# Queueing the sums of activated chunks behind the splits of the next three weight pieces

## The chip, the core and the metric

The kernel runs on one core of a Trainium2 chip. The metric is the device time of one execution in microseconds (us). Engine names are those of the profile: PE is TensorE (matmuls), PEld its weight loads, DVE is VectorE, ACT is ScalarE, POOL is GpSimd, and SP is SyncE, whose queue issues nearly all DMAs.

## What is computed

The reference is a trunk of two layers over 256 tokens of width 1024, in float32. Each layer has a token mixer (pooling, dilated attention, gates) and an MLP with a width-3 convolution over the tokens on the activated branch. The change touches the MLP alone:

```python
def _conv_ffn(xn, w_up, conv_w, conv_b, w_down):
    a, gval = jnp.split(xn @ w_up, 2, axis=-1)
    a = lax.conv_general_dilated(a, conv_w[:, None, :], ...) + conv_b
    return (jax.nn.gelu(a) * gval) @ w_down

def reference(x, ...):
    h = x
    for layer in range(DEPTH):
        h = h + _token_mixer(_rmsnorm(h, norm1[layer]), ...)
        h = h + _conv_ffn(_rmsnorm(h, norm2[layer]), w_up[layer], ...)
    return _rmsnorm(h, norm_f)
```

The inner width of the MLP is 2816, or 22 chunks of 128 columns.

## The kernel before

**Split weights.** Every weight is loaded in float32 and split on the chip into a high part `wh` (a rounding copy on ScalarE, L201) and a low part `wl` (the difference, on VectorE, L199). A matrix product is then three products: high by high, low by high and high by low. The class `Weights` does this for a fixed list of *pieces*, each 128 partitions by 1024 elements. A load brings two pieces (1024 KB). Three buffers hold raw loads and five hold split pieces (`RAW, BUFS, LOOK = 3, 5, 3`, L104). `W.get` (L218) hands out the next piece and, before that, has the pieces up to three further on split (`_split`, L158, and `open_next`, L178); `W.free` gives a piece back. A load is issued on SP as soon as a raw buffer is free, unless it is held behind another DMA (`loads_behind`, L134).

**The order.** The program is written as one stream. The compiler's scheduler places each instruction in the in-order queue of its engine, and where the stream leaves it free it may place an instruction ahead of an earlier one. `tc.issue_after(inst)` binds this: what is written inside the block and runs on the engine of `inst` is queued behind `inst`, with no wait of its own.

**The MLP's steps.** The activated branch of chunks 0 to 3 is made by rows of tokens and turned round through memory (a "crossing"); from chunk 4 on, `up` (L1249) projects each chunk by itself. The value branch is made in groups of four chunks by `by_halves` (L1233) and crosses too; the last two chunks have theirs projected (L1269). From chunk 4 on the main loop (L1316) goes by pairs of chunks, nine pairs per layer:

- at chunks 4, 8, 12 and 14, half a value group: two pieces (`HALF_GROUPS`, L42), 24 matmuls at L654;
- `up(f)` and `up(f + 1)`: two pieces, 32 matmuls at L530, drawn together by `proj(x2, 2)` (L538); then the activation of each;
- from chunk 6 on, two steps of the down projection (`residual_mm`, L576), for chunks f - 6 and f - 5 (`LAG = 6`): two pieces, 24 matmuls at L572 to L574.

So the pieces run: values, 4, 5, 6, 7, down, down, values, values, 8, 9, down, down, 10, 11, and so on.

**A chunk's sum.** A projection writes one PSUM bank: the wide matmuls (`wh`, 512 columns) fill both halves and the narrow ones (`wl`, 256 columns) add to the second. `two_sums` (L517) runs the wide ones first in one pair and the narrow ones first in the next. `add_up` (L564) fetches the second half with a copy on ScalarE (L566), then adds the first half to it on VectorE (L567). Behind that come the convolution and the gelu, three more operations on ScalarE (L1259, L1273, L1277) and five on VectorE (L1260, L1263, L1274, L1278, L1282), and the split of the result (L1293, L1294). The banks come from a pool of four (`mmp`, L237), which the value products share; a half-finished value group keeps two.

When `up(4)` has drawn pieces 4 and 5, the splits of 6, 7 and the first down piece stand ahead of `add_up` in the stream. In the queues they need not.

Of the kernel before, what the change touches and what calls it, by code (L numbers as in the profile page):

```python
# [10 lines left out]
F32 = mybir.dt.float32  # L11
# [85 lines left out]
class Weights:  # L97
# [8 lines left out]
    def __init__(self, tc, pool, idle):  # L106
        self.tc, self.nc, self.pool, self.idle = tc, tc.nc, pool, idle
        self.loads, self.pieces = [], []
        self.n_loaded, self.n_split, self.n_got = 0, 0, 0
        self.raw, self.split = {}, {}  # L110
        self.live = set()
        self.behind, self.later = (), []
        self.loads_behind = {}
        self.n_scaled, self.gains = 0, None

# [10 lines left out]
    def load(self, upto):  # L126
        while self.n_loaded < min(upto, len(self.loads)):
            src, shape, tag = self.loads[self.n_loaded]
            name = f"raw{self.n_loaded}"
            if tag is None:  # L130
                t = self.pool.tile([P, *shape], F32, tag="raw", bufs=self.RAW, name=name)
            else:
                t = self.idle.tile([P, *shape], F32, tag=tag, name=name)
            held = self.loads_behind.get(self.n_loaded)  # L134
            with self.tc.issue_after(held.ins) if held else ExitStack():
                self.last = self.nc.sync.dma_start(out=t, in_=src)
            self.raw[self.n_loaded] = t
            self.n_loaded += 1

# [38 lines left out]
    def open_next(self):  # L178


        nc, i = self.nc, self.n_split
        n, cut, shape, slot = self.pieces[i]
        if slot is None:
            self.live.add(i)
            h, l = (
                self.pool.tile([P, *shape], F32R, tag=tag, bufs=self.BUFS, name=f"{tag}{i}")
                for tag in ("wh", "wl")
            )
        else:
            tag, part, of = (*slot, 0, 1)[:3]  # L190
            if part == 0:
                self.shared = self.idle.tile([P, of, 2, *shape], F32R, tag=tag, name=f"{tag}{i}")
            h, l = self.shared[:, part, 0], self.shared[:, part, 1]
        src = cut(self.raw[n])
        self.split[i] = (h, l)
        self.n_split += 1
        if i >= self.n_scaled:
            def rest():
                self.last_rest = nc.vector.tensor_sub(out=l, in0=src, in1=h.bitcast(F32))  # L199

            return [(lambda: nc.scalar.copy(out=h, in_=src), rest)]  # L201

        def scaled(j):
            k = (i * shape[0] + j) % KD
            g = self.gains[:, k : k + 1]
            return (
                lambda: nc.scalar.activation(h[:, j], src[:, j], AF.Copy, scale=g),
                lambda: nc.vector.scalar_tensor_tensor(
                    out=l[:, j], in0=src[:, j], scalar=g, in1=h[:, j].bitcast(F32),
                    op0=ALU.mult, op1=ALU.subtract,  # L210
                ),

                lambda: nc.vector.tensor_scalar_mul(h[:, j], src[:, j], g),
            )

        return [scaled(j) for j in range(shape[0])]

    def get(self, look=LOOK):  # L218
        i = self.n_got
        self.n_got += 1  # L220
        self._split(i + 1 + look)
        return i, self.split[i]

    def free(self, i):
        self.live.discard(i)
# [3 lines left out]
def encoder(ctx, tc, x, w_in, w_pool, pool_scale, w_a, w_b, w_o, norm1, norm2, w_up, conv_w,  # L229
            conv_b, w_down, rel_bias, norm_f, onehot, edges, out):  # L230
    nc = tc.nc
# [9 lines left out]
    W = Weights(tc, wpool, big)  # L241
# [18 lines left out]
    for l in range(DEPTH):  # L260
# [36 lines left out]
        for f in range(4, NF, 2):  # L297
            if f in HALF_GROUPS:
                n, j = HALF_GROUPS[f]
                W.use(rows(w_up[l], j * 512, 4, DFF + n * 512, 512))  # L300
            a = cols(w_up[l], f * P)
            if f >= 4 * NQ:
                g = cols(w_up[l], DFF + f * P)
                a = [a[0], g[0], a[1], g[1]]
# [7 lines left out]
    h = const.tile([P, 2, D], F32, name="h")  # L312
# [225 lines left out]
    def proj(x2, n=1):  # L538


        if not ready:
            pieces = [W.get() for _ in range(n)]
            ps = [mmp.tile([P, 2, S], F32, tag="mm", name="proj_ps") for _ in range(n)]
            two_sums(
                x2, KD,
                *(
                    (b, lambda k, wh=wh: wh[:, k, :], lambda k, wl=wl: wl[:, k, :])
                    for b, (_, (wh, wl)) in zip(ps, pieces)
                ),
            )  # L550
            for i, _ in pieces:
                W.free(i)
            ready.extend((b[:, 0], b[:, 1]) for b in ps)
        return ready.pop(0)

    def halves(a):

        return a.rearrange("p (t m) -> p t m", t=2)

    def in_order(a):  # L560

        return a.rearrange("p (m t) -> p t m", t=2)

    def add_up(out, sums):  # L564

        nc.scalar.copy(out=out, in_=sums[1])  # L566
        nc.vector.tensor_add(out=out, in0=sums[0], in1=out)  # L567
# [322 lines left out]
    for l in range(DEPTH):  # L890
# [21 lines left out]
        if l == 0:  # L912
            with tc.manual_schedule():
                begun = begin_values_of_x()
            x2 = first_values(*begun, keep_values)
        else:
            for g in range(NG):
                held = begun[0] if g == 0 else [W.get() for _ in range(4)]
                for t in range(2):
                    if g + t == 0:  # L920
                        ps = begun[1]
                    else:
                        ps = v_tile()
# [16 lines left out]
        for gi in range(3, -1, -1):  # L940
            w = WINDOWS[gi]
            u = sm.tile([P, 2, S + 2 * PAD], F32, tag="u", name="u")
            nc.vector.memset(u[:, :, 0:PAD], 0.0)
            nc.vector.memset(u[:, :, PAD + S :], 0.0)
            for j in range(2):
                if l == 0 and (gi, j) == (1, 0):

                    with tc.issue_after(W.last.ins):
                        next(bias)
                add_up(in_order(u[:, j, PAD : PAD + S]), [halves(a) for a in proj(x2, 1 + (l > 0))])  # L950
            cur, n = u, S + 2 * PAD
            sh = 1
            while sh < w:
                nxt = sm.tile([P, 2, S + 2 * PAD], F32, tag="us", name="us")
                n -= sh
                nc.vector.tensor_add(
                    out=nxt[:, :, 0:n], in0=cur[:, :, 0:n], in1=cur[:, :, sh : sh + n]
                )
                cur = nxt
                sh *= 2  # L960
            hw = w // 2
            o = PAD - hw
            e = edge[:, gi, 0:hw].unsqueeze(1).to_broadcast([P, 2, hw])
            nc.vector.tensor_mul(out=cur[:, :, o : o + hw], in0=cur[:, :, o : o + hw], in1=e)
            if hw > 1:
                e = edge[:, gi, hw : w - 1].unsqueeze(1).to_broadcast([P, 2, hw - 1])
                r = slice(o + S - hw + 1, o + S)
                nc.vector.tensor_mul(out=cur[:, :, r], in0=cur[:, :, r], in1=e)
            pd = sm.tile([P, 2, S], F32, tag="us", name="pd")
            nc.vector.scalar_tensor_tensor(  # L970
                out=pd, in0=cur[:, :, o : o + S], scalar=1.0 / w, in1=u[:, :, PAD : PAD + S],
                op0=ALU.mult, op1=ALU.subtract,
            )
            both = pl2[gi // 2][:, gi % 2 * 2 : gi % 2 * 2 + 2]
            ph, pl = both[:, :, 0], both[:, :, 1]
            pd = pd.rearrange("p k (m t) -> p k t m", t=2)
            nc.scalar.copy(out=ph, in_=pd)
            nc.vector.tensor_sub(out=pl, in0=pd, in1=ph.bitcast(F32))
            pooled[gi] = both
# [122 lines left out]
        for m, c in enumerate(PAIRS):  # L1102
# [7 lines left out]
            for n in range(4):  # L1110
                if m == 1:
                    next(pool_parts)
                src, rest = (halves(a) for a in proj(x2, 1 + (m != 1)))
                hd = 2 * c + n % 2
                scale = HD**-0.5 if n < 2 else 1.0
                if hd < HPG:
# [3 lines left out]
                        out=lo[:, hd], in0=src, scalar=scale, in1=hi[:, hd].bitcast(F32),  # L1120
# [3 lines left out]
                        out=lo[:, hd], in0=rest, scalar=scale, in1=lo[:, hd].bitcast(F32),  # L1124
                        op0=ALU.mult, op1=ALU.add,
                    )
                else:
# [3 lines left out]
                        out=o, in0=src, scalar=scale, in1=o, op0=ALU.mult, op1=ALU.add  # L1131
# [6 lines left out]
        for cc in HALVES:  # L1138
            ps = by_tokens(po2, 4, then=step)
# [10 lines left out]
        for cc in HALVES:  # L1150
# [4 lines left out]
            for t in range(2):  # L1155
                nc.vector.scalar_tensor_tensor(
                    out=pa[:, t, cc], in0=th[:, t], scalar=1.0, in1=pa[:, t, cc],
# [6 lines left out]
        for n, cc in enumerate(HALVES):  # L1164
            th = gate()
            ps = by_tokens(at2, 2, 2)
# [25 lines left out]
        x2 = two_parts("x", "x2")  # L1192
# [33 lines left out]
        def to_z(ps, z, but, after):  # L1226
            y = big.tile([P, 2, 4, 4, 32], F32, tag="v0", name="crossing")
            cross(ps, y, z, "crossing", but, after)
# [4 lines left out]
        def by_halves(n):  # L1233
            ps = by_tokens(x2, 4, end=2)
            yield
            by_tokens(x2, 4, ps=ps, begin=2)
            to_z(ps, z_of[n % 3], 0, W.last_rest)
            yield

        held, ps0 = entry  # L1240
# [8 lines left out]
        def up(f):  # L1249
            w0, w1, w2, b = (prm[:, l, j * NF + f : j * NF + f + 1] for j in range(4))  # L1250
            a = sm.tile([P, S], F32, tag="u", name="a")
            if f < 4:
                nc.scalar.copy(
                    out=a.rearrange("p (a j t) -> p t a j", t=2, j=32), in_=of_chunk(za, f)
                )
            else:
                add_up(in_order(a), [halves(b) for b in proj(x2, 2)])
            y = sm.tile([P, S], F32, tag="s", name="y")
            nc.scalar.activation(y, a, AF.Identity, bias=b, scale=w1)  # L1259
            nc.vector.scalar_tensor_tensor(  # L1260
# [99 lines left out]
```

## Time and profile before

| | us |
|---|---|
| runs shown, median of 3 (lowest to highest) | 879.88 (879.86 to 880.11) |
| profiled execution, its own time | 881.7 |
| its span, first to last instruction | 879.9 |
| PE busy | 857.7 (97%) |
| PEld busy | 731.4 (83%) |
| DVE busy | 663.8 (75%) |
| ACT busy | 495.7 (56%) |

The mean granted TensorE clock is 0.991 of full speed. Times in the timeline count from the span's start. A timeline row gives the start, how long the merged instructions took, the engine, the line, the operation with output and input, the count, and in brackets the idle time before it with what ended it. The MLP of layer 0 runs from about 250 to 440 us, that of layer 1 from about 684 us to the end.

### The profile page before, as it was taken

How to read it: one execution, taken by the hardware profiler on the slowest of the kernel's cores; microseconds unless marked ns; L12 is line 12 of the kernel's file. 1: busy time of each engine (PE TensorE's matmuls, PEld its weight loads, DVE VectorE, ACT ScalarE, POOL GpSimd, SP SyncE). 2: the span in 40 equal slices, each digit the busy share in tenths (PEclk: the TensorE clock that was granted, in tenths of full speed). 3: DMA queues.
4: the chain of work that ended last, by engine and by line, in shares of the span. 5: the costliest groups of instructions: out<-in, count | busy, mean ns of one | idle time of the engine just before them, and what ended most of it. 6: DMA issues, size and time to landing. Idle time of an engine off the chain costs nothing.

```text
span 879.9 us, 11813 instructions
## 1 busy us (share of the span) xinstructions
PE 857.7 (97%) x4343; PEld 731.4 (83%) x4343; DVE 663.8 (75%) x1050; ACT 495.7 (56%) x795; POOL 31.7 (4%) x98
## 2 busy tenths in 40 slices
PE   9999999999999789999999999999999997999997
PEld 7888888888888678888888888988888886788886
DVE  7998797567677587879856987783687685787894
ACT  7756554455455466667645675453554563565673
POOL 1800000000000000000000000000000000000000
PEclk9999999999999989999999999999999998999999
DMA  9676555766848637657726564747865686466741
GB/s 333 208 244 209 182 191 199 256 233 227 297 145 283 220 131 252 239 192 239 239 96 217 167 223 160 226 159 238 305 249 187 193 284 212 172 219 219 238 162 48
DMA packets 136385, 186.80 MB, mean 212 GB/s; under 512 B 5560, under 2 KB 88192, under 8 KB 136328
## 3 DMA queue, kind: packets, MB, share of 16 engines
q1 hardware_dynamic: 136168, 185.79, 62.0%
q8 instruction: 34, 0.56, 0.3%
q10 hardware_dynamic: 160, 0.27, 0.1%
q14 instruction: 23, 0.19, 0.1%
HBM read 172.39 MB, written 13.65 MB: 211 GB/s over the span
## 4 chain that ended last, share of the span: by engine, by line
PE 95%; DVE 2%; ACT 2%; DMA 0%; issue 0%; POOLq 0%; SPq 0%; POOL 0%; ACTq 0%; DVEq 0%
PE proj_ps L530 33%; PE t_ps L654 30%; PE v_ps L654 6%; PE res_ps L572 6%; PE res_ps L573 6%; PE res_ps L574 6%; PE v_ps L882 2%; PE v_ps L789 1%; PE pool_ps L530 1%; PE o_ps L1073 1%; PE s_ps L1021 1%; PE s_ps L1016 1%; PE o_ps L1069 1%; PE xt_ps L468 1%; DVE wl L199 1%; ACT y L1259 1%
## 5 line engine op out<-in xcount | busy, mean ns | idle before, releaser
L199 DVE TENSOR_TENSOR wl<-raw,wh 128x1024 fp32r<-128x1024 f32 x274 | 329.5, 1218 | 89.3 <-ACT wh L201 67.8
L201 ACT CAST wh<-raw 128x1024 fp32r<-128x1024 f32 x274 | 283.1, 1049 | 111.4 <-PE t_ps L654 45.2
L530 PE MATMUL proj_ps<-x,wh 128*128 128x512 f32 x832 | 198.7, 392 | 0.0
L654 PE MATMUL t_ps<-wh,x 128*128 128x512 f32 x576 | 180.1, 390 | 2.7 <-ACT wh L201 2.7
L530 PEld LDWEIGHTS proj_ps<-x,wh 128*128 128x128 f32 x832 | 155.8, 190 | 31.4
L654 PEld LDWEIGHTS t_ps<-wh,x 128*128 128x128 f32 x576 | 107.7, 188 | 25.7 <-ACT wh L201 3.5
L530 PE MATMUL proj_ps<-x,wl 128*128 128x256 f32 x832 | 111.2, 289 | 11.2 <-DVE wl L199 11.2
L530 PEld LDWEIGHTS proj_ps<-x,wl 128*128 128x128 f32 x832 | 108.3, 196 | 14.4 <-DVE wl L199 11.6
L654 PE MATMUL t_ps<-wl,x 128*128 128x512 f32 x288 | 112.3, 390 | 1.1 <-DVE wl L199 1.1
L572 PE MATMUL res_ps<-wh,actq 128*128 128x512 f32 (+1 forms) x184 | 70.0, 381 | 0.0
L573 PE MATMUL res_ps<-wl,actq 128*128 128x512 f32 (+1 forms) x184 | 70.0, 380 | 0.0
L574 PE MATMUL res_ps<-wh,actk 128*128 128x512 f32 (+1 forms) x184 | 69.9, 380 | 0.0
L654 PEld LDWEIGHTS t_ps<-wl,x 128*128 128x128 f32 x288 | 54.1, 188 | 13.1 <-DVE wl L199 1.9
L654 PE MATMUL t_ps<-wh,po 128*128 128x512 f32 x128 | 41.4, 395 | 0.0
L574 PEld LDWEIGHTS res_ps<-wh,actk 128*128 128x128 f32 x184 | 34.6, 188 | 6.6
L572 PEld LDWEIGHTS res_ps<-wh,actq 128*128 128x128 f32 x184 | 34.6, 188 | 6.5
L573 PEld LDWEIGHTS res_ps<-wl,actq 128*128 128x128 f32 x184 | 34.6, 188 | 6.4
L566 ACT COPY a<-proj_ps 128x256 f32<-128x256 f32 x36 | 14.0, 390 | 37.4 <-PE proj_ps L530 37.4
L567 DVE TENSOR_TENSOR a<-proj_ps,a 128x256 f32<-128x256 f32 x36 | 15.0, 420 | 24.8 <-ACT a L566 24.8
L1293 ACT CAST actq<-g 128x256 fp32r<-128x256 f32 x44 | 17.6, 401 | 24.6 <-DVE g L1282 23.9
L441 POOL TENSOR_SCALAR ss<-ss 128x1 f32<-128x1 f32 x8 | 2.0, 255 | 802.7 <-ACT junk L434 802.7
L1259 ACT ACTIVATE y<-a,prm 128x256 f32<-128x256 f32 x44 | 25.9, 597 | 8.0 <-DVE a L567 7.9
(204 smaller groups left out, 1148.3 us busy)
## 6 DMA issues: line engine op xcount, KB each, us to landing
raw<-in_w_in_dram SPq DMA_DIRECT2D x58, 1024.0 KB, 5.5
raw<-in_w_up_dram SPq DMA_DIRECT2D x44, 1024.0 KB, 6.3
raw<-in_w_down_dram SPq DMA_DIRECT2D x22, 1024.0 KB, 5.2
raw<-in_w_a_dram SPq DMA_DIRECT2D x8, 1024.0 KB
raw<-in_w_o_dram SPq DMA_DIRECT2D x8, 1024.0 KB, 7.1
crossing<-crossing SPq DMA_DIRECT2D x12, 512.0 KB, 4.3
turning<-turning SPq DMA_DIRECT2D x8, 512.0 KB, 2.7
turned_p<-turning SPq DMA_DIRECT2D x32, 128.0 KB, 3.4
```

What stands on the lines that cost most here:

```text
L199: self.last_rest = nc.vector.tensor_sub(out=l, in0=src, in1=h.bitcast(F32))
L201: return [(lambda: nc.scalar.copy(out=h, in_=src), rest)]
L530: nc.tensor.matmul(out, w(k), x, start=(steps is first and k == 0), stop=(steps is last and k == nk - 1), skip_group_check=turns["rest"],)
L566: nc.scalar.copy(out=out, in_=sums[1])
L567: nc.vector.tensor_add(out=out, in0=sums[0], in1=out)
L572: nc.tensor.matmul(ps, ah, wh, start=first, stop=False, skip_group_check=on)
L573: nc.tensor.matmul(ps, ah, wl, start=False, stop=False, skip_group_check=on)
L574: nc.tensor.matmul(ps, al, wh, start=False, stop=last, skip_group_check=on)
L654: nc.tensor.matmul(ps, x2[:, 2 * n + j, part, t, :], w[:, j, :], start=(n + m == 0), stop=(n == last and m == 5),)
L882: nc.tensor.matmul(ps[t], a[:, k, t, :], w[:, j, :], start=(k + m == 0), stop=(k == KD - 1 and m == 2),)
L1259: nc.scalar.activation(y, a, AF.Identity, bias=b, scale=w1)
L1293: nc.scalar.copy(out=ah, in_=g)
```

## The change

The class keeps the last split's two instructions, the one on ScalarE and the one on VectorE, in `last`; the names `last` (for a load) and `last_rest` (for a low part) that it had are renamed. A new `after_splits` opens an `issue_after` block for both. In `up`, from chunk 4 on, the chunk's own sum is fetched and added in such a block. Of a pair, both sums stand behind the same split, unless the second one draws pieces of its own (chunk 21). The sums of projected values (L1269) are left as they were.

```diff
@@ class Weights, __init__
+        self.last = [None, None]
...
@@ load
-                self.last = self.nc.sync.dma_start(out=t, in_=src)
+                self.last_load = self.nc.sync.dma_start(out=t, in_=src)
...
@@ open_next
-            def rest():
-                self.last_rest = nc.vector.tensor_sub(out=l, in0=src, in1=h.bitcast(F32))
-
-            return [(lambda: nc.scalar.copy(out=h, in_=src), rest)]
+            def make(n):
+                if n == 0:
+                    inst = nc.scalar.copy(out=h, in_=src)
+                else:
+                    inst = nc.vector.tensor_sub(out=l, in0=src, in1=h.bitcast(F32))
+                self.last[n] = inst
+                return inst
+
+            return [(lambda: make(0), lambda: make(1))]
...
+    def after_splits(self):
+
+        queued = ExitStack()
+        for inst in self.last:
+            queued.enter_context(self.tc.issue_after(inst.ins))
+        return queued
...
-                    with tc.issue_after(W.last.ins):
+                    with tc.issue_after(W.last_load.ins):
...
-            to_z(ps, z_of[n % 3], 0, W.last_rest)
+            to_z(ps, z_of[n % 3], 0, W.last[1])
...
@@ up
-                add_up(in_order(a), [halves(b) for b in proj(x2, 2)])
+                sums = proj(x2, 2)
+                with W.after_splits():
+                    add_up(in_order(a), [halves(b) for b in sums])
```

## The prediction

> **What bounds the kernel now.** I read the page's chain first, then who TensorE waited for, then the timeline of that place on each engine, then busy time and clock by stretches.
>
> ```profile
> PE 95%; DVE 2%; ACT 2%; DMA 0%; issue 0%; POOLq 0%; SPq 0%; POOL 0%; ACTq 0%; DVEq 0%
> ```
>
> The chain that ended last is TensorE's (PE) own work for 95% of the span. A change elsewhere is worth only what it takes out of TensorE's waits, or adds to them. TensorE's waits, longest total first (us in total, times, longest):
>
> ```profile
> PE proj_ps L530 <- DVE wl L199: 11.2, 2, 5.6
> PE t_ps L654 <- ACT wh L201: 2.7, 2, 1.4
> PE t_ps L654 <- DVE wl L199: 1.1, 2, 0.5
> ```
>
> All three wait for the two halves of a weight piece (`wh` of L201 on ScalarE, `wl` of L199 on VectorE), each twice: once per layer. Where they lie in layer 0, on TensorE:
>
> ```profile
> 297.50 3.79 PE L530 MATMUL proj_ps<-x,wh 128*128 128x512 f32 x16
> 301.12 2.07 PE L530 MATMUL proj_ps<-x,wl 128*128 128x256 f32 x16
> 308.80 3.78 PE L530 MATMUL proj_ps<-x,wl 128*128 128x256 f32 x16 [5.61 <-DVE wl L199]
> ...
> 323.97 0.73 PE L654 MATMUL t_ps<-wh,x 128*128 128x512 f32 x2 [1.34 <-ACT wh L201]
> ```
>
> The 32 matmuls from 297.50 are chunks 4 and 5, the first pair that `up` projects itself. TensorE then stands for 5.61 us before chunks 6 and 7, and again at 322.6, before the value pieces of the next step. Why the halves are late shows on ScalarE (ACT):
>
> ```profile
> 290.10 2.00 ACT L201 CAST wh<-raw 128x1024 fp32r<-128x1024 f32 x2
> 302.28 0.40 ACT L566 COPY a<-proj_ps 128x256 f32<-128x256 f32 x1 [10.19 <-PE proj_ps L530]
> ...
> 306.46 1.98 ACT L201 CAST wh<-raw 128x1024 fp32r<-128x1024 f32 x2
> ...
> 315.40 0.39 ACT L566 COPY a<-proj_ps 128x256 f32<-128x256 f32 x1 [1.34 <-PE proj_ps L530]
> ...
> 322.88 6.03 ACT L201 CAST wh<-raw 128x1024 fp32r<-128x1024 f32 x6
> ```
>
> ScalarE splits chunks 4 and 5 at 290.10, then stands 10.19 us at the head of its queue: the next instruction is the fetch of chunk 4's sum (L566), which TensorE finishes just before 302.28. The splits of chunks 6 and 7 come behind it and behind part of the activation, at 306.46. The same happens at 315.40, where the sums of 6 and 7 and their activation stand ahead of the value splits at 322.88. Their data was not what they waited for. The loads, on the queue of SP, and the median time from issue to landing:
>
> ```profile
> 289.27 0.39 SPq L136 DMA_DIRECT2D raw<-in_w_up_dram  x1
> 291.36 0.39 SPq L136 DMA_DIRECT2D raw<-in_w_down_dram  x1
> ...
> 301.30 9.00 SPq L136 DMA_DIRECT2D raw<-in_w_up_dram  x2
> ```
>
> ```profile
> raw<-in_w_up_dram SPq DMA_DIRECT2D x44, 1024.0 KB, 6.3
> raw<-in_w_down_dram SPq DMA_DIRECT2D x22, 1024.0 KB, 5.2
> ```
>
> Chunks 6 and 7 are one load, issued at 289.27, so landed near 295.6; the first two down pieces, issued at 291.36, near 296.6. The wait is one of order, and the order is what the change sets.
>
> The wait costs more than its length. The stretches are: length, busy time of PE, PEld, DVE, ACT and POOL, granted clock, DMA share, GB/s.
>
> ```profile
> 297.50:303.20 5.70, 5.69 (x33) 4.87 (x31) 0.42 (x1) 0.43 (x2) 0.00 (x0) 1.00 0.46 123
> ...
> 308.80:317.00 8.20, 8.20 (x32) 7.30 (x33) 5.72 (x10) 3.86 (x7) 0.00 (x0) 0.65 0.71 247
> ...
> 346.00:357.00 11.00, 11.00 (x50) 9.09 (x49) 10.02 (x18) 9.44 (x15) 0.00 (x0) 1.00 0.31 108
> ```
>
> ```profile
> 742.75:750.75 8.00, 8.00 (x32) 7.16 (x33) 5.73 (x10) 3.85 (x7) 0.00 (x0) 0.67 0.72 244
> ```
>
> ```profile
> 330.53 5.54 PE proj_ps L530 x32
> ```
>
> The same 32 matmuls take 5.54 us unhindered (last row, from the chain), but 8.20 us right behind the wait in layer 0 and 8.00 us in layer 1, at a granted clock of 0.65 and 0.67. So the wait loses a further 8.20 - 5.54 = 2.66 and 8.00 - 5.54 = 2.46 us.
>
> What could be removed at most: 11.2 + 2.7 + 1.1 = 15.0 us of waits and 2.66 + 2.46 = 5.1 us of slow clock, 20.1 us in all.
>
> The clock loss sets against a rule of the Trainium skill. Its page "TensorE: Matmul & The Clock Gate", section "What's actually happening", has the clock halved after an idle window of about 3.4 us and full again after as long a busy one. By that rule a wait would lose some 3.4 / 2 = 1.7 us, an estimate from that page, and the removable sum would be 18.4 us instead of 20.1. The trace has 2.66 and 2.46, and I go by the trace.
>
> **The change, part by part.** No instruction is added or dropped: the new `last` pair only renames, and the load and the crossing that used `last` and `last_rest` keep what they were ordered behind. What moves is `add_up` of the chunk's own sum: its copy on ScalarE is queued behind the newest `wh`, its addition on VectorE behind the newest `wl`. When chunks 4 and 5 have been drawn, these belong to chunks 6, 7 and the first down piece. Both queues are in order, so these three splits now come before 302.28.
>
> Can they run there? Each costs what the group rows say:
>
> ```profile
> L199 DVE TENSOR_TENSOR wl<-raw,wh 128x1024 fp32r<-128x1024 f32 x274 | 329.5, 1218 | 89.3 <-ACT wh L201 67.8
> L201 ACT CAST wh<-raw 128x1024 fp32r<-128x1024 f32 x274 | 283.1, 1049 | 111.4 <-PE t_ps L654 45.2
> ```
>
> From 295.6 on, three times 1.05 us on ScalarE ends near 298.8, and 1.22 us of VectorE behind the last near 300.0. The third also needs the buffer (there are five) of the value piece that TensorE leaves just before 297.50; with some 0.3 us for the last matmul's end (an estimate: 3.79 us for 16 matmuls that start within 3.62) its halves run to 298.9 and 300.1. The sum is there at 302.28. So the moved splits cost nothing there: the idle time of 10.19 us covers them, and has 2 us to spare. If the loads land later than that, the sums move by the excess, and TensorE still has chunks 6 and 7.
>
> What is late next is the PSUM bank. The pool has four, and two are held by the half-finished values from chunk 4 to chunk 8, so chunks 6 and 7 must take the banks of 4 and 5. VectorE frees them here:
>
> ```profile
> 302.71 0.42 DVE L567 TENSOR_TENSOR a<-proj_ps,a 128x256 f32<-128x256 f32 x1 [7.57 <-ACT a L566]
> ...
> 304.20 0.42 DVE L567 TENSOR_TENSOR a<-proj_ps,a 128x256 f32<-128x256 f32 x1
> ```
>
> Chunk 4's bank is free at 303.13, before TensorE ends chunk 5 at 301.12 + 2.07 = 303.19. Chunk 7's eight narrow matmuls come eight after that, 8 x 2.07 / 16 = 1.0 us, at 304.2; its bank is free at 304.62, and 0.1 for the signal makes a new wait of 0.5 us per layer. If both copies go back to back it is nothing. I take 0.5: 1.0 in all. That is too short to bring the clock down: the wait of 1.34 above is followed by matmuls at the usual pace.
>
> The second place: the sums of 6 and 7 go behind the first value piece (load issued 301.30, behind the crossing; landed near 301.30 + 6.3 = 307.6). The wide matmuls go at (301.12 - 297.50) / 16 = 0.226 us. TensorE ends chunk 6 (narrow ones first this time, then its eight wide) near 303.7 + 2.07 + 1.8 = 307.6 and chunk 7 near 303.7 + 5.5 = 309.2. The split first takes 1.05 us, so the first sum is fetched at 307.7 to 308.7, up to 1.0 us late. The new wait holds ScalarE and VectorE, and with them the activation of 4 and 5 if that isn't through; its consumer, the down pieces of 6 and 7, comes three steps later, so nobody waits. TensorE then does two down pieces of twelve such matmuls and stands before the values at about 309.2 + 5.4 = 314.6, before the second of them at 316.0 (six matmuls on). If that second piece is split after the whole activation, as at 322.88, 7.5 us after the first sum at 315.40, it is begun at 315.2 to 316.2, and its second half is there 2.3 us later: TensorE waits 1.3 to 2.3 us, against (2.7 + 1.1) / 2 = 1.9 now. If it falls in between, as the splits at 306.46 did, nothing is left. I take 0.8 per layer, nearer to that row, because here too the data will have landed while the activation runs: 1.6 in all.
>
> Further on, the required split precedes the sum already, or can. At chunk 10 it doesn't:
>
> ```profile
> 345.33 0.39 ACT L566 COPY a<-proj_ps 128x256 f32<-128x256 f32 x1
> ...
> 349.20 1.99 ACT L201 CAST wh<-raw 128x1024 fp32r<-128x1024 f32 x2
> ```
>
> ```profile
> 337.19 0.96 SPq L136 DMA_DIRECT2D raw<-in_w_up_dram  x2
> ```
>
> Its value piece, loaded at 337.19, has landed by 343.5, so ScalarE's half is made by 344.6 and VectorE's by 345.8, where the copy ends at 345.72 and the addition comes behind it. I count 0.
>
> Sum: 20.1 - 1.0 - 1.6 = 17.5 us less. From the profiled execution, 881.7 - 17.5 = 864.2; the median of the runs shown is 1.8 us below that execution, so 879.88 - 17.5 = 862.4 us.
>
> **The rivals.** *Given back later.* TensorE arrives some 9 us earlier per layer at the steps from chunk 8 on, where VectorE was busy 10.02 of 11.00 us (346 to 357). An order with the activation ahead of a needed split would give one wait a layer like today's, 1.9 to 5.6 us: 862.4 + 3.8 to 862.4 + 11.2, so 866 to 874. For it: VectorE's fill. Against it: three splits a layer are made 10 us earlier, so VectorE has less left, and the waits above have no place from chunk 8 on.
>
> *Nothing happens.* The three splits can't go ahead, for a load or a buffer, and 880 remains. Against it: the landing near 296 and the buffers above.
>
> *Slower: the sums starve VectorE.* In each of the nine pairs a layer the copy and addition stand in line until a load has landed and is split. VectorE has 1.0 us to spare in a pair (11.00 - 10.02); beyond that a wait goes to TensorE. Losing the 17.5 us and 1.8 more over 18 pairs takes 1.1 us each, so it decides from waits of 2.1 us per pair; at 3 us each the time is 862.4 + 18 x 2 = 898. Against it: chunk 10 above, where the split can be made in time, at 0.1 us.
>
> The skill's page "PSUM — Partial Sum Buffer", section "Engine vs sequencer instructions", calls the queues of ScalarE and VectorE strictly first in, first out. That is what both this rival and the gain rest on; the 10.19 us row agrees.
>
> **How the numbers follow.** Forecast (both waits mostly gone, 859.5 to 865.5) 0.72; given back later, 0.16; nothing happens, 0.04; slower, 0.05; more than 20.1 us gained, 0.03. The time is 862.4. The range starts at 859, all 20.1 us gone and a little, and ends at 869, in the middle of the second case. A measurement can tell about 0.2%, 1.8 us, from no change: faster 0.91, same 0.04, slower 0.05.
>
> **What would show it.** Right: two or three L201 rows on ScalarE between 294 and 300, no wait of proj_ps for `wl`, clock 1.00 over chunks 6 and 7, 32 matmuls in 5.5 to 6.1 us, the wait at L530 now on L567 and below 1 us. Wrong: TensorE waits from chunk 8 on, a L566 that waits for `wh` or DMA with VectorE idle, or splits of 6 and 7 still behind 302.

## The result and the profile after

| | before | after |
|---|---|---|
| median of 4 runs (lowest to highest), us | 879.87 (879.79 to 880.11) | 860.13 (859.81 to 860.34) |
| profiled execution, its own time, us | 881.7 | 859.81 |
| span of that execution, us | 879.9 | 858.0 |
| mean granted TensorE clock in it | 0.991 | 0.998 |

The ratio is 0.9775 (0.9758 to 0.9792): 19.7 us less in the medians, where 17.5 was forecast. The profiled executions differ by 21.9: that of the kernel before took 1.8 us more than its median, that of the changed kernel 0.3 us less.

Line numbers shift in the new kernel: L136 is now L137, L199 is L203 (L201 stays), L530 is L543, L566 and L567 are L579 and L580, L572 to L574 are L585 to L587, and L654 is L667. The engines' shares of the chain that ended last, then the one entry in the list of TensorE's waits (us in total, times, longest):

```profile
PE 99%; DVE 0%; ACT 0%; POOL 0%; issue 0%; POOLq 0%; ACTq 0%
```

```profile
PE gain_ps L372 <- PEq L1357: 0.8, 1, 0.8
```

The one wait left is at the very start. Both places of the MLP are gone from the list, in both layers. ScalarE and TensorE at chunk 4 of layer 0:

```profile
295.24 2.00 ACT L201 CAST wh<-raw 128x1024 fp32r<-128x1024 f32 x2 [3.50 <-DMA raw<-in_w_up_dram]
299.29 1.05 ACT L201 CAST wh<-raw 128x1024 fp32r<-128x1024 f32 x1 [2.04 <-DMA raw<-in_w_down_dram]
301.92 0.39 ACT L579 COPY a<-proj_ps 128x256 f32<-128x256 f32 x1 [1.58 <-PE proj_ps L543]
302.88 0.39 ACT L579 COPY a<-proj_ps 128x256 f32<-128x256 f32 x1 [0.57 <-PE proj_ps L543]
...
309.94 1.05 ACT L201 CAST wh<-raw 128x1024 fp32r<-128x1024 f32 x1
310.89 0.66 ACT L579 COPY a<-proj_ps 128x256 f32<-128x256 f32 x2
311.43 1.05 ACT L201 CAST wh<-raw 128x1024 fp32r<-128x1024 f32 x1
```

```profile
300.77 2.08 PE L543 MATMUL proj_ps<-x,wl 128*128 128x256 f32 x16
302.68 0.63 PE L585 MATMUL res_ps<-wh,actq 128*128 128x512 f32 x2
303.15 0.39 PE L586 MATMUL res_ps<-wl,actq 128*128 128x512 f32 x1
303.38 2.07 PE L543 MATMUL proj_ps<-x,wl 128*128 128x256 f32 x16
305.29 3.82 PE L543 MATMUL proj_ps<-x,wh 128*128 128x512 f32 x16
```

Three splits stand where ScalarE stood idle, and now wait for their loads instead; 1.58 us of spare time is left on ScalarE before the first sum. Chunks 6 and 7 start at 303.38, where they started at 308.80. The value piece of chunk 8 is split at 309.94, ahead of the sums of 6 and 7, and its second piece at 311.43, ahead of their activation. Between chunks 5 and 6 TensorE now does three matmuls of the down projection: its order has changed too, most likely because the scheduler laid out the stream anew with the first down piece split early. The stretch of chunks 6 and 7 (the same columns as before):

```profile
303.38:308.90 5.52, 5.52 (x33) 4.91 (x32) 4.77 (x11) 3.44 (x7) 0.00 (x0) 1.00 0.99 331
```

It takes 5.52 us at full clock, where it took 8.20 us at 0.65.

Nearly all of the gain lies between the first matmul of chunk 4 and the first of chunk 8, 112 matmuls in each layer (the counts below take in one or two at the edges). The two layers before, then the two after:

```profile
297.50:330.37 32.87, 25.39 (x114) 21.02 (x112) 22.33 (x38) 17.75 (x30) 0.00 (x0) 0.90 0.43 143
731.46:764.10 32.64, 25.17 (x114) 20.88 (x113) 22.34 (x38) 17.73 (x30) 0.00 (x0) 0.90 0.43 142
```

```profile
297.14:319.14 22.00, 22.00 (x113) 18.84 (x112) 17.62 (x32) 14.88 (x27) 0.00 (x0) 1.00 0.72 252
720.21:742.21 22.00, 22.00 (x114) 18.85 (x112) 18.44 (x32) 15.72 (x27) 0.00 (x0) 1.00 0.75 259
```

That is 10.87 + 10.64 = 21.5 of the 21.9 us between the profiled executions. By the starts of the matmuls, chunks 6 and 7 account for 2.66 + 2.44 = 5.1 us of it, the slow clock; the other 16.4 us are the waits.

### The profile page after: what moved, and what is told of

It reads as the page before. It is cut to its first block, busy times and chain, and to the rows that moved or that the text cites. A ratio compares the mean times of both kernels' runs of the same rounds, so it can differ in the third digit from the quotient of the medians.

```text
span 858.0 us, 11823 instructions
## 1 busy us (share of the span) xinstructions
PE 851.6 (99%) x4343; PEld 727.9 (85%) x4343; DVE 661.2 (77%) x1050; ACT 493.8 (58%) x795; POOL 32.0 (4%) x98
## 4 chain that ended last, share of the span: by engine, by line
PE 99%; DVE 0%; ACT 0%; POOL 0%; issue 0%; POOLq 0%; ACTq 0%
PE proj_ps L543 34%; PE t_ps L667 30%; PE v_ps L667 6%; PE res_ps L586 6%; PE res_ps L585 6%; PE res_ps L587 6%; PE v_ps L895 3%; PE v_ps L802 1%; PE pool_ps L543 1%; PE o_ps L1086 1%; PE s_ps L1034 1%; PE s_ps L1029 1%; PE o_ps L1082 1%; PE xt_ps L481 1%; PE gain_ps L372 0%; PE xt_ps L750 0%
## 5 line engine op out<-in xcount | busy, mean ns | idle before, releaser
L203 DVE TENSOR_TENSOR wl<-raw,wh 128x1024 fp32r<-128x1024 f32 x274 | 329.8, 1217 | 88.1 <-ACT wh L201 73.6
L201 ACT CAST wh<-raw 128x1024 fp32r<-128x1024 f32 x274 | 284.3, 1049 | 118.3 <-PE t_ps L667 49.0
L543 PE MATMUL proj_ps<-x,wh 128*128 128x512 f32 x832 | 196.9, 390 | 0.0
L543 PEld LDWEIGHTS proj_ps<-x,wh 128*128 128x128 f32 x832 | 154.3, 188 | 30.9
L667 PE MATMUL t_ps<-wh,x 128*128 128x512 f32 x576 | 179.7, 390 | 0.0
L667 PEld LDWEIGHTS t_ps<-wh,x 128*128 128x128 f32 x576 | 107.8, 188 | 22.3
L667 PE MATMUL t_ps<-wl,x 128*128 128x512 f32 x288 | 112.1, 389 | 0.0
L543 PEld LDWEIGHTS proj_ps<-x,wl 128*128 128x128 f32 x832 | 105.4, 191 | 3.0
L543 PE MATMUL proj_ps<-x,wl 128*128 128x256 f32 x832 | 107.8, 283 | 0.0
L587 PE MATMUL res_ps<-wh,actk 128*128 128x512 f32 (+1 forms) x184 | 69.9, 380 | 0.0
L585 PE MATMUL res_ps<-wh,actq 128*128 128x512 f32 (+1 forms) x184 | 69.7, 381 | 0.0
L667 PEld LDWEIGHTS t_ps<-wl,x 128*128 128x128 f32 x288 | 54.1, 188 | 11.2
L667 PE MATMUL t_ps<-wh,po 128*128 128x512 f32 x128 | 41.4, 395 | 0.0
L587 PEld LDWEIGHTS res_ps<-wh,actk 128*128 128x128 f32 x184 | 34.6, 188 | 6.6
L585 PEld LDWEIGHTS res_ps<-wh,actq 128*128 128x128 f32 x184 | 34.5, 188 | 6.3
L667 PEld LDWEIGHTS t_ps<-wh,po 128*128 128x128 f32 x128 | 24.0, 188 | 4.9
L447 ACT ACTIVATE junk<-h 128x512 f32<-128x512 f32 (+1 forms) x19 | 10.5, 553 | 28.6 <-DVE h L445 28.5
L579 ACT COPY a<-proj_ps 128x256 f32<-128x256 f32 x36 | 13.6, 389 | 23.3 <-PE proj_ps L543 23.3
```

Source lines behind the costliest of these rows:

```text
L201: inst = nc.scalar.copy(out=h, in_=src)
L203: inst = nc.vector.tensor_sub(out=l, in0=src, in1=h.bitcast(F32))
L447: nc.scalar.activation(junk[:, 0 : cc.stop - cc.start], h[:, t, cc], AF.Square, scale=D**-0.5, accum_out=ss[:, n : n + 1],)
L543: nc.tensor.matmul(out, w(k), x, start=(steps is first and k == 0), stop=(steps is last and k == nk - 1), skip_group_check=turns["rest"],)
L585: nc.tensor.matmul(ps, ah, wh, start=first, stop=False, skip_group_check=on)
L587: nc.tensor.matmul(ps, al, wh, start=False, stop=last, skip_group_check=on)
```

## The experiments

The kernel before was run again beside each group; its medians were 881.31 (first four experiments), 880.58 (next four) and 881.06 us (last four). Ratios are to these.

**Only chunks 4 and 5.**

```diff
-                with W.after_splits():
+                with W.after_splits() if f in (4, 5) else ExitStack():
```

> Only the sums of chunks 4 and 5 stand behind the splits. Theory (two separate places per layer, each a matter of order on ScalarE): the wait of 5.6 us before chunks 6 and 7 and the slow clock behind it are gone, the wait before the value pieces of chunk 8 stays, at 1.3 to 2.9 us a layer: 862.7 to 866 us. Rival (the order of the later steps matters too): nearer to 870, with waits of TensorE from chunk 8 on. Rival (one cause, and the second wait only follows from the first): 860.1 and no wait.

Measured: 869.06 us, ratio 0.9869 (0.9854 to 0.9884), 3 us above the expected band. TensorE's waits and the stretch behind the wait in layer 0:

```profile
PE t_ps L667 <- ACT wh L201: 3.7, 2, 1.8
...
PE t_ps L667 <- DVE wl L203: 1.0, 2, 0.5
```

```profile
318.00:324.74 6.74, 6.74 (x23) 5.37 (x23) 5.87 (x7) 4.14 (x5) 0.00 (x0) 0.75 0.60 203
```

The first place is mended and the second stays, as the theory has it, with 4.7 us of waits. What it missed is the clock: 0.75 over 6.74 us, a loss of 6.74 x 0.25 = 1.7 us in that layer, and 0.79 over 6.38 us, 1.3 us, in the other. Together they are the 3 us. In the kernel before, the second wait had no slow clock behind it.

**Only chunks 6 and 7** (the same line with `f in (6, 7)`).

> Only the sums of chunks 6 and 7 stand behind the splits. Theory: the first wait and its slow clock stay as before, the second wait of 1.9 us a layer goes: 875.5 to 876.5 us. Rival (the second wait only follows from the first): 879.9, with both waits.

Measured: 877.4 us, ratio 0.9962 (0.9949 to 0.9974), 3.9 us under its kernel before and 0.9 us above the expected band.

```profile
PE proj_ps L543 <- DVE wl L203: 11.2, 2, 5.6
PE t_ps L667 <- DVE wl L203: 1.1, 2, 0.6
```

```profile
308.52:317.00 8.48, 8.47 (x33) 7.49 (x34) 6.77 (x10) 4.21 (x7) 0.00 (x0) 0.64 0.71 246
741.10:748.50 7.40, 7.39 (x33) 6.72 (x34) 6.37 (x10) 4.12 (x7) 0.00 (x0) 0.75 0.67 230
```

The first wait is whole and the second is gone from its place. The 1.1 us is a new one, before the values of chunk 12. So the two places are separate matters of order. Against the 5.54 us of an unhindered pair the slow stretch loses 2.9 us in one layer and 1.9 in the other: the same wait doesn't always cost the same clock.

**Only the addition on VectorE.**

```diff
-        for inst in self.last:
+        for inst in self.last[1:]:
```

> Only the addition on VectorE stands behind the low part's split; the copy on ScalarE is free, and the scheduler puts it ahead of the splits of chunks 6, 7 and the first down piece. Theory (ScalarE's order decides): the high parts come after the copies, from 302.3 or 303.2 on, the first wait stays at 3 to 6 us with slow clock, the second goes or shrinks: 872 to 878 us. Rival (VectorE, the fuller engine, decides): 860 to 862.

Measured: 875.37 us, ratio 0.994 (0.9922 to 0.9959). ScalarE, then TensorE's waits in the MLP:

```profile
302.41 0.39 ACT L579 COPY a<-proj_ps 128x256 f32<-128x256 f32 x1 [10.18 <-PE proj_ps L543]
303.36 0.38 ACT L579 COPY a<-proj_ps 128x256 f32<-128x256 f32 x1 [0.57 <-PE proj_ps L543]
303.64 3.88 ACT L201 CAST wh<-raw 128x1024 fp32r<-128x1024 f32 x4
```

```profile
PE res_ps L585 <- ACT wh L201: 6.6, 2, 3.3
PE res_ps L586 <- DVE wl L203: 1.7, 2, 0.9
```

ScalarE stands at the first copy for 10.18 us again, and the splits begin at 303.64. VectorE's order, though right, waits for ScalarE's. TensorE still waits 8.3 us, now before the down matmuls ahead of chunk 6, and runs behind it at a clock of 0.68 over 7.94 us in layer 0. So the half on ScalarE is needed: VectorE's alone gains 5.9 of some 20 us. Whether ScalarE's alone would do wasn't tried.

**The first wait filled.** Matmuls whose result nobody reads are put into the kernel before.

```diff
+                if f == 4:
+                    fill = v_tile()
+                    with tc.issue_after(turns["end"].ins):
+                        for n in range(25):
+                            nc.tensor.matmul(
+                                fill, x2[:, n % KD, 0, 0, :], x2[:, n % KD], start=True, stop=True
+                            )
```

> The kernel before, with 25 matmuls of no use put on TensorE between chunk 5 and chunk 6, so that it is busy through the first wait; the splits stay late. Theory (the wait costs its length and a slow clock behind it): the clock stays at 1.00, chunks 6 and 7 take 5.5 us and not 8.2 or 8.0, and the time falls by up to 5.1 us, to 874.8. By half a window of 3.4 us per layer (the Trainium skill, TensorE: Matmul & The Clock Gate, section What's actually happening) it would be 876.5. Rival (chunks 6 and 7 are slow for another reason, such as their low parts coming late one by one): 879 to 881, and chunks 6 and 7 still at 8 us.

Measured: 880.13 us, ratio 0.9986 (0.9976 to 0.9997): 1.2 us instead of 5.1.

```profile
308.30:313.90 5.60, 5.60 (x33) 4.87 (x33) 5.21 (x9) 3.51 (x8) 0.00 (x0) 1.00 0.90 304
...
322.50:329.20 6.70, 6.69 (x22) 5.41 (x23) 5.21 (x5) 3.54 (x4) 0.00 (x0) 0.75 0.68 243
```

Chunks 6 and 7 do run at full clock, so the idle time was the cause. But in this execution the slow stretch has moved behind the second wait, 0.75 over 6.70 us. Neither theory had that: one wait hid what the other would cost. It doesn't cost the same each time: over the ten runs the time went from 878.09 to 881.28 us and the mean clock from 0.994 to 0.999, and the fastest run had the highest clock.

**Only from chunk 8 on** (`f >= 8`).

> Only the sums from chunk 8 on stand behind the splits (seven of nine pairs a layer). Theory: both waits stay, and the new order of the later steps neither gains nor costs: 879 to 881 us. Rival (a part of the gain comes from the later steps): 865 to 875. Rival (the waits of the sums cost something there, which the gain at chunks 4 and 6 hides): 882 or more.

Measured: 881.89 us (880.06 to 886.5), ratio 1.0023 (1.0006 to 1.004). Both waits stand as before and nothing is gained. The two longest runs, 885.68 and 886.5 us, had the lowest mean clocks, 0.989 and 0.987; they weren't profiled, and the cause of the small loss stays open.

**Only chunks 4 to 7** (`f < 8`), and the same again beside the changed kernel.

> Only the sums of chunks 4 to 7 stand behind the splits. Theory: these two pairs are the whole gain: 859.5 to 861 us and no wait of TensorE. Rival (the later steps add or cost): 862 or more, or 858.5 or less.

> Only the sums of chunks 4 to 7 behind the splits, beside the changed kernel on the same chip. Theory (the binding at chunk 10 keeps a wait away, before the value pieces of chunk 12, that the shifted order would bring): 0.93 - 0.23 = 0.7 us a layer, so 1.4 us above the changed kernel. Rival (the difference of 1.7 us seen before is one between chips): within 0.4 us.

> The changed kernel once more, beside the next one. 860.1 us and no wait of TensorE, spread below 1 us.

Measured: 861.87 us, ratio 0.9787 (0.9772 to 0.9801); again 862.49, ratio 0.9791 (0.9776 to 0.9805), beside 860.86 for the changed kernel, ratio 0.9773 (0.9758 to 0.9788). The first is 0.9 us above what was expected of it, with a wait where none was. The intervals overlap, so the times alone don't settle the 1.6 us. The traces of both runs show what the changed kernel hasn't:

```profile
PE t_ps L667 <- DVE wl L203: 1.1, 2, 0.5
```

That is again the wait before the values of chunk 12, 0.5 us of it per layer by the profile: with the sums and the activation of chunk 10 ahead of the value split, the early order is late there. The changed kernel, which binds from chunk 8 on too, splits first there and has no such wait; that the binding at chunk 10 alone does it wasn't tried. The changed kernel's own second profile (861.82 us, in a spread of 1.9 us where less than 1 was expected) shows how thin the cover at chunk 4 can be; ScalarE, SP and TensorE:

```profile
299.87 2.00 ACT L201 CAST wh<-raw 128x1024 fp32r<-128x1024 f32 x2 [6.92 <-DMA raw<-in_w_up_dram]
302.58 1.05 ACT L201 CAST wh<-raw 128x1024 fp32r<-128x1024 f32 x1 [0.72 <-DMA raw<-in_w_down_dram]
303.53 0.67 ACT L579 COPY a<-proj_ps 128x256 f32<-128x256 f32 x2
```

```profile
294.10 0.39 SPq L137 DMA_DIRECT2D raw<-in_w_up_dram  x1
```

```profile
303.68 0.73 PE L585 MATMUL res_ps<-wh,actq 128*128 128x512 f32 x2 [0.56 <-ACT wh L201]
304.94 0.50 PE L586 MATMUL res_ps<-wl,actq 128*128 128x512 f32 x1 [0.53 <-DVE wl L203]
```

Here the load of 6 and 7 was issued at 294.10 in place of 289.53, and the third split, begun at 302.58, ended behind the end of chunk 5 at 303.12. The three down matmuls that now stand ahead of chunk 6 need that third piece, and TensorE waits 0.56 and 0.53 us.

**Two pieces instead of three** (the last split is noted after the pair's first `get`).

```diff
+            pieces = [W.get()]
+            W.two = list(W.last)
+            pieces += [W.get() for _ in range(n - 1)]
```

> The sums stand behind two further pieces and not three: for chunk 4 behind 6 and 7, for chunk 6 behind the two down pieces. Theory: the first wait goes, since 6 and 7 are what TensorE needs next, and the second comes back, since the value piece is the third at chunk 6: 862.7 to 866 us, as with only chunks 4 and 5 bound. Rival (any two pieces ahead do, TensorE is covered): 860 to 861.

Measured: 871.13 us, ratio 0.989 (0.9875 to 0.9905), 5 us above the expected band. The first wait is gone; the second is back and longer. Behind it comes a slow clock in layer 0, and none in layer 1:

```profile
PE t_ps L669 <- ACT wh L201: 5.6, 2, 2.8
```

```profile
318.70:325.30 6.60, 6.60 (x23) 5.32 (x24) 5.51 (x6) 3.80 (x4) 0.00 (x0) 0.76 0.64 218
747.38:752.52 5.14, 5.14 (x22) 4.24 (x23) 5.14 (x6) 3.74 (x4) 0.00 (x0) 1.00 0.51 156
```

So it matters that it is three: the third piece at chunk 6 is the value piece.

**Four pieces.**

```diff
                 sums = proj(x2, 2)
+                W._split(W.n_got + 4)
```

> The sums stand behind four further pieces. The fourth at chunk 4 needs the split buffers of chunk 4, so the sums are fetched about 1.5 us later than they are there. Theory (what is late next is the PSUM bank of chunks 4 and 5): TensorE waits 0.5 to 1.3 us a layer before chunks 6 and 7, unless the scheduler puts enough down matmuls in between: 860 to 862.7 us. Rival (waiting sums starve VectorE in each pair): 2 us and more in each pair from chunk 8 on, 880 or more.

Measured: 860.75 us, ratio 0.9776 (0.9762 to 0.9791), no wait of TensorE in the MLP. The scheduler set five down matmuls between chunks 5 and 6, and the banks were free in time. Sums behind one more split starve nothing here, which speaks against the forecast's slower rival.

**Both waits filled, and the second only partly.** As in the first fill, and 11 or 4 such matmuls behind the down piece before chunk 8.

```diff
+            if f == 8:
+                fill = mmp.tile([P, 512], F32, tag="mm", name="fill_ps")
+                with tc.issue_after(turns["down"].ins):
+                    for n in range(11):
...
```

> The kernel before with both waits of a layer filled by matmuls of no use: 25 before chunk 6 and 11 before the values of chunk 8 (2.5 us). Theory (the waits cost their length, and one stretch of slow clock per layer comes behind whichever wait leaves TensorE idle for some 2 us or more): no slow clock is left, and only the filled lengths remain above the kernel after: 860.1 + 2 x (5.6 + 2.2) = 875.7 us, 4 to 5 us under the kernel before. Rival (the slow clock has another cause than the idle time): 879 to 881, with a stretch at a clock of about 0.75.

> As with both waits filled, but only 4 matmuls (0.9 us) in the second, so that TensorE stands there for about 1.0 and 0.7 us. Theory (a wait of about 1 us is too short to bring the clock down, as the wait of 1.7 and 0.7 us was in the kernel before): 875.7 us as with both filled, clock 1.00 behind it. Rival (every wait there brings the clock down once the first one doesn't): 879 to 881.

Measured: 877.72 us, ratio 0.9964 (0.9951 to 0.9977), with 11; 877.94, ratio 0.9966 (0.9955 to 0.9978), with 4. Both lie 2 us above the forecast sum. The stretches from chunk 4 to chunk 8 with 11, in both layers, then the waits with 4, and the stretch behind them in layer 0:

```profile
297.41:328.02 30.61, 30.61 (x149) 25.43 (x148) 22.08 (x38) 17.68 (x30) 0.00 (x0) 1.00 0.46 152
729.67:760.26 30.59, 30.59 (x150) 25.41 (x148) 22.08 (x38) 17.69 (x30) 0.00 (x0) 1.00 0.53 174
```

```profile
PE t_ps L654 <- ACT wh L201: 1.3, 2, 0.7
PE t_ps L654 <- DVE wl L199: 1.1, 2, 0.5
```

```profile
322.50:329.20 6.70, 6.56 (x29) 5.45 (x30) 6.49 (x8) 3.95 (x5) 0.00 (x0) 1.00 0.65 231
```

No slow clock in either. Filling is worth 881.06 - 877.72 = 3.3 us. That is less than the clock loss, because the filled stretches are 30.61 + 30.59 - 44.00 = 17.2 us longer than those of the changed kernel, 0.8 us more than the 16.4 us of the waits: so the fills put the clock loss at some 3.3 + 0.8 = 4.1 us.

## Why the prediction was right, and where its terms were off

- **What bounds the kernel, and that order is the cause**: right. Each place alone goes when its own sums are bound (chunks 4 and 5; chunks 6 and 7) and stays when they aren't; without the binding of ScalarE's copy most of the gain is lost.
- **The waits, 15.0 us**: 1.4 us too small. The list of waits counts the time in which no matmul runs; by the starts of the matmuls the waits hold 16.4 us (per layer 5.77 us for 5.61 before chunk 6, and 2.44 for 1.87 before the values).
- **The slow clock, 5.1 us**: right in kind, and right for the execution that it was read from. Other executions lose less: 2.9 + 1.9 us with only chunks 6 and 7 bound and 2.3 + 1.9 us with binding only from chunk 8 on, and the fills give some 4.1 us. The estimate from the Trainium skill ("TensorE: Matmul & The Clock Gate", "What's actually happening"), 1.7 us a layer or 3.4 in all, is lower than each of these. The idle window of 3.4 us in the same section of the Trainium skill isn't what the runs show as a threshold for a single wait: 1.84 and 0.53 us sufficed in one run, and 2.79 and 0.53 us brought nothing down in one layer of another. That the loss is bound to the first wait was wrong: when the first is gone, the second can bring it. So was the step that a wait of 1.34 us is too short, as a rule: 1.56 and 0.53 us brought the clock down in the first fill.
- **The PSUM bank, 1.0 us taken**: nothing, and so no new wait on L567, which was named as a sign. VectorE frees chunk 5's bank at 303.72, and with three down matmuls ahead chunk 7 needs it only at about 304.3.
- **The second place, 1.6 us taken**: nothing. Both value pieces are split before the activation of 6 and 7. (The upper branch of the working has a slip: 315.2 to 316.2 and 2.3 us more, less 316.0, is a wait of 1.5 to 2.5 us, not 1.3 to 2.3.)
- **Chunk 10, counted 0**: right for the kernel as it is. Without binding from chunk 8 on, 0.5 us a layer is waited there.
- **Loads landed in time**: right, but with less to spare than forecast. The down load, issued at 291.01, let its split begin only at 299.29, 8.3 us later, where 5.2 us was taken. The third split ends at 300.34 on ScalarE and 301.59 on VectorE, for 298.9 and 300.1 in the working, and the sum is fetched at 301.92. In another profile it isn't in time, and that costs 1.1 us.

Put right by the runs, the forecast gain of 17.5 us grows by the 2.6 us of the two costs that weren't there and by the 1.4 us that the waits hold more: 21.5 us, which is what the two stretches lose between the profiled executions. The medians differ by 19.7 us, chiefly because the profiled execution of the kernel before took 1.8 us more than its median. The forecast took terms from that long execution off the shorter median, and this offset part of the costs that didn't come: so the nearness of 17.5 to 19.7 is in part luck. Up to 1.0 us of the 1.8 may be slow clock (5.1 there, 4.1 by the fills); the rest stays open.

## What to carry to other kernels

An engine that stands idle at the head of its in-order queue, while work with its data landed stands behind, is a matter of order: bind the waiting instruction behind that work, and go as far as the piece that the bound engine needs next. Price two neighbouring waits together, since mending one can let the other bring the clock down. Measure a wait by the starts of the instructions around it too, since its entry in the list of waits can be too small. Check the spare time of each moved step in more than one execution: here a load issued 4.6 us later used it up.

## What the runs showed of the hardware

A mean clock over a stretch hides two levels. In shorter windows the clock behind the first wait of the kernel before is 0.50, and then 1.00:

```profile
312.00:313.00 1.00, 1.00 (x5) 0.90 (x5) 1.00 (x2) 0.00 (x0) 0.00 (x0) 0.50 1.08 385
314.00:315.00 1.00, 1.00 (x5) 0.74 (x4) 0.42 (x1) 0.06 (x1) 0.00 (x0) 0.77 0.66 196
315.00:316.00 1.00, 1.00 (x6) 0.82 (x5) 0.18 (x1) 0.39 (x1) 0.00 (x0) 1.00 1.06 438
```

So TensorE ran at half clock from the end of that wait, 308.80, to about 314.4, for some 5.6 us. With the first fill alone the half clock lasted some 3.4 us, from about 322.9 to 326.3, which shows as 0.75 over 6.70 us. It came there after waits of 1.6 and 0.5 us:

```profile
PE t_ps L654 <- ACT wh L201: 3.1, 2, 1.6
PE t_ps L654 <- DVE wl L199: 1.1, 2, 0.5
```

The clock stayed at 1.00 after 0.7 and 0.5 us, and in layer 0 of the kernel before after 1.34 and 0.53 us, with a slow stretch shortly ahead:

```profile
325.20:330.30 5.10, 5.07 (x22) 4.21 (x23) 5.10 (x5) 3.57 (x4) 0.00 (x0) 1.00 0.54 178
```

Neither the length of the wait nor an earlier slow stretch explains all of this. With two pieces, TensorE waited 2.79 and some 0.5 us in each layer of the same execution; behind it the clock fell in layer 0 and stayed at 1.00 in layer 1, with no slow stretch in the 6 us ahead of the wait in either layer. What decides between them stays open.
